# A batched matrix product: weights cast to bfloat16 by their own transfers instead of by VectorE and ScalarE

## The chip, the cores and the metric

The kernel runs on one NeuronCore of a Trainium2 chip. The metric is the device time of one execution in microseconds; inputs and output lie in the chip's main memory (HBM), in float32, before and after. A core has five engines that run on their own and meet at semaphores: PE (TensorE, matrix products), DVE (VectorE), ACT (ScalarE), POOL (GpSimd) and SP (SyncE, which issues transfers here). Sixteen DMA engines carry out the transfers.

## The reference

```python
b1, b2, m, k, n = 8, 16, 256, 512, 384
x      = np.random.randn(b1, b2, m, k).astype(np.float32)
weight = np.random.randn(b1, b2, k, n).astype(np.float32)

def reference(x, weight):
    return np.matmul(x, weight).astype(np.float32)
```

These are 128 independent products of a 256 x 512 with a 512 x 384 matrix. x has 67.1 MB, weight 100.7 MB, the result 50.3 MB.

## The kernel before

The 128 products are taken in 32 groups (NG) of four (G). The matrix products are computed from bfloat16 copies of x and weight, with sums in float32.

**x.** One transfer of 2048 KB (load_x, L104) brings a group's four matrices of 256 x 512 into x_sb, 128 partitions with eight rows of 512 each: partitions 0 to 31 hold the first matrix, and so on. There are two such buffers. In four steps of two rows (T = 4, the index q in the code) DVE casts them to x_bf (cast_x, L142), which has one buffer; PE transposes x_bf into PSUM, two bfloat16 values taken as one 32-bit word (transpose, L193); ACT copies the transposed words to x_t (evacuate, L183), which has two buffers.

**Weights.** One transfer of 3072 KB (load_w, L116) brings a group's four matrices into w_sb as float32, with 16 adjacent rows (24 KB) in each partition: partitions 0 to 31 hold the first matrix. There are two buffers. Each matmul needs a whole matrix spread over 128 partitions, four rows in each. So the casts to w_bf also move data between partitions: 16 casts for a group (cast_w, L154), each from 32 partitions with 4 rows to 32 other partitions. DVE does 11 of them (CV) and ACT 5 (CA). w_bf holds two groups. In the first four groups and the last two ("short" groups, is_short, L113) a group comes in two transfers of 1536 KB with 8 rows in each partition, and DVE alone makes 8 casts of 64 partitions (cast_short, L167).

Since the rows of a matrix fall on partitions in another order this way (which row of K stands where), cast_x writes the columns of x in a matching order: its output or input is rearranged by S = 4, or S = 2 in the short groups.

**Products.** For each step q PE multiplies two sets of rows (multiply, L208): the four matrices of a group use 32 columns of the array each, and four matmuls follow one another over K. That is 128 matmuls of 384 columns in a group, into one of two PSUM buffers (po). ACT copies po to out_sb (copy_out, L228), four buffers; one transfer of 1536 KB stores a group (store, L132).

**Order.** The order of every engine is written out by hand.

- SP issues all transfers from one queue (on_sync, L244): first x and weights of four groups (LAG), then for each group: load_x of group n + 4, store of group n, load_w of group n + 4. A load waits until the casts of the group two earlier have freed its buffer: L108 waits for x_cast, L120 and the line behind it for w_vcast and w_acast.
- DVE (on_vector, L266) takes for each group 8 weight casts, the four x casts of the next group, and the last 3 weight casts.
- PE (on_tensor, L294) transposes group n + 1, then multiplies group n.
- ACT (on_scalar, L309) evacuates the transposes of group n + 1, then copies group n's results out in four steps with 5 weight casts of group n + 1 between them.
- POOL (on_gpsimd, L238) makes the identity matrix for the transposes and has nothing else to do.

Of the kernel before, what the change touches and what calls it, by code (L numbers as in the profile page):

```python
# [12 lines left out]
def kernel(  # L13
# [6 lines left out]
    nc = tc.nc  # L20
    P = 128
# [20 lines left out]
    C = P // G  # L42
    R = G * M // P
    T = R // 2
    SH, SL = 2, 4
    NG = B // G

    XS, WS, OS = 2, 2, 4
    BS, TS, WBS = 1, 2, 2 * G
    PT, PO = 4, 2  # L50

    LAG = 4

    CA = 5
    CV = G * SL - CA
    HV = G * SH

    XV = 8

    ctx.enter_context(tc.tile_critical(no_gpsimd_drain=True))  # L60

# [10 lines left out]
    def sems(name, n):  # L72
        return [tc.alloc_semaphore(f"{name}{s}") for s in range(n)]
# [4 lines left out]

    x_bf = sbuf("x_bf", [P, R, K], bf16, BS)
    x_t = sbuf("x_t", [P, R, KO // 2, P, 2], bf16, TS)  # L80
    w_sb = sbuf("w_sb", [P, SL * KO, N], fp32, WS)
    w_bf = sbuf("w_bf", [P, KO, N], bf16, WBS)
    out_sb = sbuf("out_sb", [P, R, N], fp32, OS)
    pt = psum("pt", [P, 2, KO // 2, P], fp32, PT)
    po = psum("po", [P, 2, 512], fp32, PO)
# [1 line left out]

    id_done, x_cast, w_vcast, w_acast, t_made, t_copied, p_made, o_copied = (  # L90
        sems(name, 1)[0]
        for name in (
            "id_done", "x_cast", "w_vcast", "w_acast",
            "t_made", "t_copied", "p_made", "o_copied",
        )
    )
    x_in, w_in, o_out = sems("x_in", XS), sems("w_in", WS), sems("o_out", OS)
    h_in = sems("h_in", G)


    BIAS = 8
# [8 lines left out]
            x_rows[bass.ds(n * (G * M), G * M)].rearrange("(p r) k -> p r k", r=R),  # L110
        ).then_inc(x_in[s % XS], 16)

    def is_short(n):  # L113
        return isinstance(n, int) and (n < LAG or n >= NG - 2)

    def load_w(e, t, U, s):  # L116
        n = t * U + s
        if not isinstance(n, int) or n >= WS:
            e.wait_ge(w_vcast, n * CV + (1 - WS) * CV)
            e.wait_ge(w_acast, n * CA + (1 - WS) * CA)  # L120
        d = SL // SH if is_short(n) else 1
        k = SL * KO // d
        for h in range(d):
            sem = h_in[s % WS * 2 + h] if is_short(n) else w_in[s % WS]
            e.dma_start(  # L125
                w_sb[s % WS][:, h * k : (h + 1) * k, :],
                w_rows[bass.ds(n * (G * K) + h * (G // d * K), G // d * K)].rearrange(
                    "(p k) n -> p k n", k=k
                ),
            ).then_inc(sem, 16)  # L130

    def store(e, t, U, s, pieces=1):  # L132
        n = t * U + s
# [8 lines left out]
    def cast_x(e, t, U, s, q):  # L142
        n = t * U + s
        if q == 0:
            e.wait_ge(x_in[s % XS], (t * (U // XS) + s // XS) * 16 + 16)
        e.wait_ge(t_made, n * T + (q + 1 - T + BIAS))  # L146
        rows = slice(2 * q, 2 * q + 2)
        S = SH if is_short(n) else SL
        e.tensor_copy(  # L149
            out=x_bf[s % BS][:, rows].rearrange("p r (s q c) -> p r s q c", s=S, c=KO),  # L150
            in_=x_sb[s % XS][:, rows].rearrange("p r (q s c) -> p r s q c", s=S, c=KO),
        ).then_inc(x_cast, 1)

    def cast_w(e, t, U, s, parts, first=True):  # L154
        n = t * U + s
        if first:
            e.wait_ge(p_made, n * T + (BIAS - T))
            e.wait_ge(w_in[s % WS], (t * (U // WS) + (s - LAG) // WS) * 16 + 16)  # L158
        copy = e.tensor_copy if e is nc.vector else e.copy
        for c in parts:  # L160
            i, h = c // SL, c % SL
            copy(  # L162
                out=w_bf[(s * G + i) % WBS][h * C : (h + 1) * C],
                in_=w_sb[s % WS][i * C : (i + 1) * C, h * KO : (h + 1) * KO, :],
            ).then_inc(w_vcast if c < CV else w_acast, 1)

    def cast_short(e, n):  # L167
        e.wait_ge(p_made, n * T + (BIAS - T))
        p = P // SH
        for d in range(SL // SH):  # L170
            turns = n // WS if n < LAG else LAG // WS
            e.wait_ge(h_in[n % WS * 2 + d], turns * 16 + 16)  # L172
            for a in range(SH):
                for h in range(SH):
                    c = d * 4 + a * 2 + h
                    r = (d * SH + h) * KO

                    e.tensor_copy(  # L178
                        out=w_bf[(n * G + d * SH + a) % WBS][h * p : (h + 1) * p],
                        in_=w_sb[n % WS][a * p : (a + 1) * p, r : r + KO, :],  # L180
                    ).then_inc(w_vcast, 2 if c < CV - HV else 1)

    def evacuate(e, t, U, s):  # L183
        n = t * U + s
# [22 lines left out]

    def multiply(e, t, U, s):  # L208
        n = t * U + s
        e.wait_ge(w_acast, n * CA + CA)  # L210
        e.wait_ge(w_vcast, n * CV + CV)
        for q in range(T):
            e.wait_ge(t_copied, n * T + (q + 1 + BIAS))
            e.wait_ge(o_copied, n * T + (q + 1 - PO + BIAS))
            for rr in range(2):
                for ko in range(KO):
                    for i in range(G):
                        mine = slice(i * C, (i + 1) * C)
                        ins = e.matmul(  # L219
                            po[(s * T + q) % PO][mine, rr, :N],  # L220
                            x_t[s % TS][:, 2 * q + rr, ko // 2, mine, ko % 2],
                            w_bf[(s * G + i) % WBS][:, ko, :],
                            start=(ko == 0),
                            stop=(ko == KO - 1),
                        )
            ins.then_inc(p_made, 1)
# [11 lines left out]
    def on_gpsimd(e):  # L238
# [2 lines left out]
        make_identity(nc, identity[:], nomemset=True)  # L241
        e.drain().then_inc(id_done, 1)

    def on_sync(e):  # L244
        U = OS
        for n in range(LAG):
            load_x(e, 0, NG, n)
            load_w(e, 0, NG, n)
        rounds = (NG - 2 - LAG) // U
        with e.Fori(0, rounds) as t:  # L250
            for s in range(U):
                load_x(e, t, U, LAG + s)
                store(e, t, U, s)
                load_w(e, t, U, LAG + s)

        for n in range(LAG + rounds * U, NG):
            load_x(e, 0, NG, n)
            if n < NG - 1:
                store(e, 0, NG, n - LAG)
            load_w(e, 0, NG, n)  # L260
        for n in range(NG - 1 - LAG, NG):
            store(e, 0, NG, n, T if n == NG - 1 else 1)
        for s in range(OS):
            e.wait_ge(o_out[s], 16 + 16 * (NG // OS + (T - 1 if s == (NG - 1) % OS else 0)))

    def on_vector(e):  # L266
        U = 2

        def next_x(t, U, s):
            for q in range(T):  # L270
                cast_x(e, t, U, s + 1, q)

        def step(t, U, s):
            n = t * U + s
            if is_short(n):
                cast_short(e, n)
            else:
                cast_w(e, t, U, s, range(XV))
            if not isinstance(n, int) or n < NG - 1:
                next_x(t, U, s)  # L280
            if not is_short(n):
                cast_w(e, t, U, s, range(XV, CV), False)

        next_x(0, NG, -1)
        for n in range(LAG):
            step(0, NG, n)
        rounds = (NG - 3 - LAG) // U
        with e.Fori(0, rounds) as t:  # L288
            for s in range(U):
                step(t, U, LAG + s)  # L290
        for n in range(LAG + rounds * U, NG):
            step(0, NG, n)

    def on_tensor(e):  # L294
        U = 2
        e.sem_inc(t_made, BIAS)
        e.sem_inc(p_made, BIAS)
        e.wait_ge(id_done, 2)
# [1 line left out]

        pe = mybir.EngineType.PE
        with nc.Fori(0, NG // U, engines=OrderedEngineSet([pe]), head_slot={pe: 0}) as t:
            transpose(e, t, U, 1)
            multiply(e, t, U, 0)
            with e.If(t < NG // U - 1):
                transpose(e, t, U, 2)
            multiply(e, t, U, 1)

    def on_scalar(e):  # L309
        U = OS  # L310
# [4 lines left out]

        def step(t, U, s):
            short = is_short(t * U + s + 1)
            evacuate(e, t, U, s + 1)  # L320
            for q in range(T):
                copy_out(e, t, U, s, q)
                if q == 0 and short:
                    e.sem_inc(w_acast, CA)
                if q > 0 and not short:
                    last = CA if q == T - 1 else q
                    cast_w(e, t, U, s + 1, range(CV + q - 1, CV + last), q == 1)

        evacuate(e, 0, NG, 0)
        e.sem_inc(w_acast, CA)  # L330
        for n in range(LAG - 1):
            step(0, NG, n)
        rounds = (NG - 2 - LAG) // U
        with e.Fori(0, rounds) as t:
            for s in range(LAG - 1, LAG - 1 + U):
                step(t, U, s)
        for n in range(LAG - 1 + rounds * U, NG - 1):
            step(0, NG, n)
        for q in range(T):
            copy_out(e, 0, NG, NG - 1, q)  # L340

    on_gpsimd(nc.gpsimd)
    on_sync(nc.sync)
    on_vector(nc.vector)
    on_tensor(nc.tensor)
# [31 lines left out]
```

## Time and profile before

| | |
|---|---|
| time, median of 2 runs | 518.49 us (518.36 to 518.61) |
| profiled execution: span from the first to the last instruction | 516.8 us |
| granted clock of PE, mean over the span | 0.780 of full speed |
| busy: PE / DVE / ACT / POOL | 315.2 / 397.7 / 410.3 / 0.7 us |
| DMA: moved / rate over the span | 218.19 MB / 422 GB/s |
| transfers: weights, x, results | 26 of 3072 KB and 12 of 1536 KB, 32 of 2048 KB, 31 of 1536 KB and 4 of 384 KB |

The profile is of one execution, and its own time is the span; the runs of the first row were timed apart from it, and their median is 1.7 us more. Busy time is the time in which an engine executes; an engine can be idle because it waits, which is no harm unless all the rest waits for it. The trace also records each packet that a DMA engine moves, with its size and the time that it took; here a packet is one contiguous run of one partition. In the groups of instructions a line such as "L162 DVE CAST w_bf<-w_sb 32x1536 bf16<-32x1536 f32 x286 | 271.9, 951 | 81.6" is to be read: line 162 of the kernel, executed by DVE, a cast from w_sb to w_bf of 32 partitions by 1536 values, 286 times, 271.9 us in all, 951 ns each, and 81.6 us idle ahead of them.

### The profile page before, as it was taken

Reading aid. Unit: us, or ns where it says so; the run is one execution under the profiler, and the core shown is the slowest. Engines: PE = TensorE matmul, PEld = TensorE weight load, DVE = VectorE, ACT = ScalarE, POOL = GpSimd, SP = SyncE. Lnnn points to the kernel's source line nnn. Section 1 sums busy time; section 2 is a strip of 40 time slices with the busy share of each in tenths; the row PEclk is TensorE's granted clock in tenths of the full one; section 3 lists DMA queues with packets and bytes.
Section 4 is the critical chain, followed back from the end, with each engine's and each line's share of the span. In section 5 each row is a group of like instructions: output and inputs, shape, how many; then the busy total and the mean of one; then the engine's idle time right before and its main releaser. Section 6 shows DMA issues by size and latency. Waiting matters only on the chain.

```text
span 516.8 us, 11572 instructions
## 1 busy us (share of the span) xinstructions
PE 315.2 (61%) x4608; PEld 225.4 (44%) x4608; DVE 397.7 (77%) x462; ACT 410.3 (79%) x387; POOL 0.7 (0%) x6
## 2 busy tenths in 40 slices
PE   2277838555676675765475766558656667565681
PEld 2255525444454443454353544435534445344550
DVE  2788757798777897777987778977779777797960
ACT  1365666998797989798979879978989897899561
POOL 0000000000000000000000000000000000000000
PEclk9687786878786778787778868776867786688887
DMA  8999999999999999999999999999999999999995
GB/s 335 426 428 425 435 429 423 431 430 434 429 424 431 432 439 434 424 426 433 434 434 431 422 432 433 435 429 428 425 438 429 440 428 420 433 433 429 424 428 219
DMA packets 15127, 218.19 MB, mean 422 GB/s; under 512 B 1680, under 2 KB 1680, under 8 KB 2192
## 3 DMA queue, kind: packets, MB, share of 16 engines
q1 hardware_dynamic: 15120, 218.11, 99.0%
q8 instruction: 3, 0.05, 0.0%
q14 instruction: 4, 0.03, 0.0%
HBM read 167.77 MB, written 50.33 MB: 422 GB/s over the span
## 4 chain that ended last, share of the span: by engine, by line
DMA 57%; DVE 29%; issue 9%; PE 1%; SPq 1%; DVEq 1%; ACT 0%
DMA w_sb<-in_weight_dram 57%; DVE w_bf L162 20%; DVE x_bf L149 5%; DVE w_bf L178 4%; PE po L219 1%; SPq L125 0%; DVEq L288 0%; SPq L108 0%; DVEq L158 0%; ACT out_sb L233 0%; SPq L120 0%; DVEq L146 0%; DVEq L172 0%; SPq L372 0%; SPq L60 0%
## 5 line engine op out<-in xcount | busy, mean ns | idle before, releaser
L162 DVE CAST w_bf<-w_sb 32x1536 bf16<-32x1536 f32 x286 | 271.9, 951 | 81.6 <-DMA w_sb<-in_weight_dram 73.5
L219 PE MATMUL po<-w_bf,x_t 128*32 128x384 bf16 x4096 | 200.6, 359 | 38.3 <-DVE w_bf L162 21.0
L201 PE MATMUL pt<-identity,x_bf 128*128 128x128 f32 x512 | 115.0, 415 | 152.2 <-DVE x_bf L149 152.2
L162 ACT CAST w_bf<-w_sb 32x1536 bf16<-32x1536 f32 x130 | 190.9, 1468 | 6.0 <-DMA w_sb<-in_weight_dram 2.8
L201 PEld LDWEIGHTS pt<-identity,x_bf 128*128 128x128 f32 x512 | 103.4, 224 | 164.1 <-issue 163.8
L219 PEld LDWEIGHTS po<-w_bf,x_t 128*32 128x32 bf16 x4096 | 122.0, 106 | 115.9 <-issue 40.7
L233 ACT COPY out_sb<-po 128x768 f32<-128x768 f32 x128 | 101.5, 803 | 57.3 <-PE po L219 56.6
L188 ACT COPY x_t<-pt 128x1024 bf16<-128x1024 bf16 x128 | 120.3, 1025 | 22.1 <-PE pt L201 21.5
L149 DVE CAST x_bf<-x_sb 128x1024 bf16<-128x1024 f32 x128 | 80.0, 688 | 12.4 <-DMA x_sb<-in_x_dram 11.5
L178 DVE CAST w_bf<-w_sb 64x1536 bf16<-64x1536 f32 x48 | 45.9, 955 | 8.3 <-DMA w_sb<-in_weight_dram 7.0
L188 ACT ACT_TABLE_LOAD x1 | 1.3, 1283 | 10.8 <-PE pt L201 10.8
masks.py:199 POOL TENSOR_SCALAR_AFFINE_SELECT identity<-identity 128x128 f32<-128x128 f32 x1 | 0.3, 294 | 0.2 <-POOL identity L239 0.2
L239 POOL MEMSET identity<- 128x128 f32 x1 | 0.2, 205 | 0.5 <-SPq L60 0.5
L361 POOL MEMSET const-bfloat16-1.0<- 128x1 bf16 x1 | 0.1, 102 | 0.0
L361 POOL MEMSET const-uint8-127<- 128x1 uint8 x1 | 0.1, 102 | 0.0
L361 POOL MEMSET const-float32-0.0<- 128x1 f32 x1 | 0.1, 99 | 0.2 <-issue 0.2
L361 POOL MEMSET const-float32-1.0<- 128x1 f32 x1 | 0.1, 99 | 0.0
## 6 DMA issues: line engine op xcount, KB each, us to landing
w_sb<-in_weight_dram SPq DMA_DIRECT2D x26, 3072.0 KB, 18.1
x_sb<-in_x_dram SPq DMA_DIRECT2D x32, 2048.0 KB, 22.3
out_dram<-out_sb SPq DMA_DIRECT2D x31, 1536.0 KB, 25.4
w_sb<-in_weight_dram SPq DMA_DIRECT2D x12, 1536.0 KB, 16.6
out_dram<-out_sb SPq DMA_DIRECT2D x4, 384.0 KB, 5.6
```

The source lines that it names most:

```text
L149: e.tensor_copy(out=x_bf[s % BS][:, rows].rearrange("p r (s q c) -> p r s q c", s=S, c=KO), in_=x_sb[s % XS][:, rows].rearrange("p r (q s ...
L162: copy(out=w_bf[(s * G + i) % WBS][h * C : (h + 1) * C], in_=w_sb[s % WS][i * C : (i + 1) * C, h * KO : (h + 1) * KO, :],).then_inc(w_vcas ...
L178: e.tensor_copy(out=w_bf[(n * G + d * SH + a) % WBS][h * p : (h + 1) * p], in_=w_sb[n % WS][a * p : (a + 1) * p, r : r + KO, :],).then_inc ...
L188: e.copy(out=x_t[s % TS][:, 2 * q : 2 * q + 2], in_=pt[(s * T + q) % PT][:].bitcast(bf16),).then_inc(t_copied, 1)
L201: ins = e.transpose(pt[(s * T + q) % PT][:, rr, h, :], words[:, 2 * q + rr, h :: KO // 2], identity[:],)
L219: ins = e.matmul(po[(s * T + q) % PO][mine, rr, :N], x_t[s % TS][:, 2 * q + rr, ko // 2, mine, ko % 2], w_bf[(s * G + i) % WBS][:, ko, :], ...
L233: e.copy(out=out_sb[s % OS][:, 2 * q : 2 * q + 2, :], in_=po[(s * T + q) % PO][:, :, :N],).then_inc(o_copied, 1)
L239: e.memset(identity[:], 0.0).then_inc(id_done, 1)
L361: nc = _bacc.Bacc("TRN2", target_bir_lowering=False, num_devices=1)
```

## The change

Weight transfers are issued from GpSimd, and source and destination differ in type: they read float32 from HBM and write bfloat16 into w_bf. w_sb and all weight casts of DVE and ACT are gone, and with them the short groups. w_bf is one tensor for a group, 128 partitions with four rows of each of the four matrices, in two buffers; partition p holds rows 4p to 4p + 3 of each matrix. Since that is the order in which x has its columns, cast_x casts without rearranging. load_w of group n + 2 waits until PE has finished the products of group n; GpSimd issues all 32 after it has made the identity matrix. multiply waits for the transfer's semaphore instead of the casts'. On SP the loop now has the store of group n, then load_x of group n + 4.

```diff
-    XS, WS, OS = 2, 2, 4
-    BS, TS, WBS = 1, 2, 2 * G
+    XS, OS = 2, 4
+    BS, TS, WBS = 1, 2, 2
...
-    w_sb = sbuf("w_sb", [P, SL * KO, N], fp32, WS)
-    w_bf = sbuf("w_bf", [P, KO, N], bf16, WBS)
+    w_bf = sbuf("w_bf", [P, G, KO, N], bf16, WBS)
...
+    def load_w(e, n):
+        if n >= WBS:
+            e.wait_ge(p_made, (n + 1 - WBS) * T + BIAS)
+        e.dma_start(
+            w_bf[n % WBS][:],
+            w_rows[bass.ds(n * (G * K), G * K)].rearrange("(g p k) n -> p g k n", g=G, p=P),
+        ).then_inc(w_in[n % WBS], 16)
...
-        S = SH if is_short(n) else SL
-        e.tensor_copy(
-            out=x_bf[s % BS][:, rows].rearrange("p r (s q c) -> p r s q c", s=S, c=KO),
-            in_=x_sb[s % XS][:, rows].rearrange("p r (q s c) -> p r s q c", s=S, c=KO),
-        ).then_inc(x_cast, 1)
+        e.tensor_copy(out=x_bf[s % BS][:, rows], in_=x_sb[s % XS][:, rows]).then_inc(x_cast, 1)
...
     def multiply(e, t, U, s):
         n = t * U + s
-        e.wait_ge(w_acast, n * CA + CA)
-        e.wait_ge(w_vcast, n * CV + CV)
+        e.wait_ge(w_in[s % WBS], (t * (U // WBS) + s // WBS) * 16 + 16)
...
-                            w_bf[(s * G + i) % WBS][:, ko, :],
+                            w_bf[s % WBS][:, i, ko, :],
...
+    def load_all_w(e):
+        for n in range(NG):
+            load_w(e, n)
...
     def on_sync(e):
         U = OS
         for n in range(LAG):
             load_x(e, 0, NG, n)
-            load_w(e, 0, NG, n)
-        rounds = (NG - 2 - LAG) // U
+        rounds = (NG - LAG) // U
         with e.Fori(0, rounds) as t:
             for s in range(U):
+                store(e, t, U, s)
                 load_x(e, t, U, LAG + s)
-                store(e, t, U, s)
-                load_w(e, t, U, LAG + s)
...
     def on_vector(e):
         U = 2
+        with e.Fori(0, NG // U) as t:
             for s in range(U):
+                for q in range(T):
+                    cast_x(e, t, U, s, q)
...
+        evacuate(e, 0, NG, 0)
+        rounds = (NG - U) // U
+        with e.Fori(0, rounds) as t:
+            for s in range(U):
+                evacuate(e, t, U, s + 1)
+                for q in range(T):
+                    copy_out(e, t, U, s, q)
...
     on_gpsimd(nc.gpsimd)
+    load_all_w(nc.gpsimd)
```

More of the change, by code (lines that the diff above doesn't have):

```diff
@@ L44 @@
     T = R // 2
-    SH, SL = 2, 4
     NG = B // G
-    XS, WS, OS = 2, 2, 4
-    BS, TS, WBS = 1, 2, 2 * G
+    XS, OS = 2, 4
+    BS, TS, WBS = 1, 2, 2
     PT, PO = 4, 2
     LAG = 4
[L54 to L58, printed above, removed]
     ctx.enter_context(tc.tile_critical(no_gpsimd_drain=True))
@@ L85 @@
     po = psum("po", [P, 2, 512], fp32, PO)
-    id_done, x_cast, w_vcast, w_acast, t_made, t_copied, p_made, o_copied = (
+    id_done, x_cast, t_made, t_copied, p_made, o_copied = (
         sems(name, 1)[0]
         for name in (
-            "id_done", "x_cast", "w_vcast", "w_acast",
+            "id_done", "x_cast",
             "t_made", "t_copied", "p_made", "o_copied",
@@ L96 @@
     )
-    x_in, w_in, o_out = sems("x_in", XS), sems("w_in", WS), sems("o_out", OS)
-    h_in = sems("h_in", G)
+    x_in, w_in, o_out = sems("x_in", XS), sems("w_in", WBS), sems("o_out", OS)
     BIAS = 8
@@ L111, in load_x @@
         ).then_inc(x_in[s % XS], 16)
[L113 to L130, printed above, removed]
+    def load_w(e, n):
[5 more added lines that the diff above has]
+        ).then_inc(w_in[n % WBS], 16)
     def store(e, t, U, s, pieces=1):
@@ L147, in cast_x @@
         rows = slice(2 * q, 2 * q + 2)
-        S = SH if is_short(n) else SL
-        e.tensor_copy(
-            out=x_bf[s % BS][:, rows].rearrange("p r (s q c) -> p r s q c", s=S, c=KO),
-            in_=x_sb[s % XS][:, rows].rearrange("p r (q s c) -> p r s q c", s=S, c=KO),
-        ).then_inc(x_cast, 1)
[L154 to L181, printed above, removed]
+        e.tensor_copy(out=x_bf[s % BS][:, rows], in_=x_sb[s % XS][:, rows]).then_inc(x_cast, 1)
     def evacuate(e, t, U, s):
@@ L247, in on_sync @@
             load_x(e, 0, NG, n)
-            load_w(e, 0, NG, n)
-        rounds = (NG - 2 - LAG) // U
+        rounds = (NG - LAG) // U
         with e.Fori(0, rounds) as t:
             for s in range(U):
+                store(e, t, U, s)
                 load_x(e, t, U, LAG + s)
-                store(e, t, U, s)
-                load_w(e, t, U, LAG + s)
[L256 to L261, printed above, removed]
+        for n in range(NG - LAG, NG):
             store(e, 0, NG, n, T if n == NG - 1 else 1)
@@ L267, in on_vector @@
         U = 2
[L269 to L288, printed above, removed]
+        with e.Fori(0, NG // U) as t:
             for s in range(U):
-                step(t, U, LAG + s)
-        for n in range(LAG + rounds * U, NG):
-            step(0, NG, n)
+                for q in range(T):
+                    cast_x(e, t, U, s, q)
     def on_tensor(e):
-        U = 2
+        U = WBS
         e.sem_inc(t_made, BIAS)
@@ L302, in on_tensor @@
         with nc.Fori(0, NG // U, engines=OrderedEngineSet([pe]), head_slot={pe: 0}) as t:
-            transpose(e, t, U, 1)
-            multiply(e, t, U, 0)
+            for s in range(U - 1):
+                transpose(e, t, U, s + 1)
+                multiply(e, t, U, s)
             with e.If(t < NG // U - 1):
-                transpose(e, t, U, 2)
-            multiply(e, t, U, 1)
+                transpose(e, t, U, U)
+            multiply(e, t, U, U - 1)
     def on_scalar(e):
@@ L314, in on_scalar @@
             e.sem_inc(o_out[s], 16)
-        def step(t, U, s):
-            short = is_short(t * U + s + 1)
-            evacuate(e, t, U, s + 1)
-            for q in range(T):
[L322 to L340, printed above, removed]
+        evacuate(e, 0, NG, 0)
[5 more added lines that the diff above has]
+                    copy_out(e, t, U, s, q)
+        for n in range(rounds * U, NG):
+            if n < NG - 1:
+                evacuate(e, 0, NG, n + 1)
+            for q in range(T):
+                copy_out(e, 0, NG, n, q)
     on_gpsimd(nc.gpsimd)
+    load_all_w(nc.gpsimd)
     on_sync(nc.sync)
```

## The prediction

> **What bounds the kernel now.** I read the page's share of the DMA queues first, then the table of windows, then the chain of waits, and last the groups of instructions. The queue part of the page:
>
> ```profile
> q1 hardware_dynamic: 15120, 218.11, 99.0%
> HBM read 167.77 MB, written 50.33 MB: 422 GB/s over the span
> ```
>
> The reader is to see 99.0%: all loads and stores run on one queue, and their packets fill the 16 DMA engines for 0.99 of 516.8 us. The bytes are exactly those of x, weight and out; nothing is moved twice. The windows say where the missing 1% lies (columns: window, its length, busy us and count of each engine, clock, DMA share, GB/s):
>
> ```profile
> 0.00:20.00 20.00, 3.46 (x16) 3.28 (x16) 8.61 (x11) 5.04 (x5) 0.70 (x6) 0.90 0.91 366
> 200.00:300.00 100.00, 59.14 (x894) 43.02 (x884) 82.59 (x96) 90.26 (x84) 0.00 (x0) 0.79 1.01 432
> 500.00:517.00 17.00, 5.39 (x128) 3.77 (x128) 0.10 (x1) 3.20 (x4) 0.00 (x0) 0.83 0.63 262
> ```
>
> DMA stands at 1.01 in the middle (full), 0.91 in the first 20 us (1.8 us lost) and 0.63 in the last 17 us (6.3 us lost). The chain of waits seems to say something else:
>
> ```profile
> DMA 57%; DVE 29%; issue 9%; PE 1%; SPq 1%; DVEq 1%; ACT 0%
> ```
>
> 29% of it is DVE, because SP issues a weight load only when the casts have freed w_sb, so the chain passes through casts. But while those casts run the DMA engines have other transfers, which the window row of 1.01 shows. A cast that vanishes therefore gives its time to nobody. The groups that the change removes or touches (busy us, mean ns, idle before):
>
> ```profile
> L162 DVE CAST w_bf<-w_sb 32x1536 bf16<-32x1536 f32 x286 | 271.9, 951 | 81.6 <-DMA w_sb<-in_weight_dram 73.5
> L162 ACT CAST w_bf<-w_sb 32x1536 bf16<-32x1536 f32 x130 | 190.9, 1468 | 6.0 <-DMA w_sb<-in_weight_dram 2.8
> L149 DVE CAST x_bf<-x_sb 128x1024 bf16<-128x1024 f32 x128 | 80.0, 688 | 12.4 <-DMA x_sb<-in_x_dram 11.5
> L178 DVE CAST w_bf<-w_sb 64x1536 bf16<-64x1536 f32 x48 | 45.9, 955 | 8.3 <-DMA w_sb<-in_weight_dram 7.0
> ```
>
> **The price of a packet.** The trace records every DMA packet with its size and time. Medians: 3072 B in 121 ns, 12288 B in 460, 16384 B in 612, 24576 B in 912. From the first and the second, 9216 B take 339 ns, 27.2 B per ns; what is left is 8 ns a packet (24576 / 27.2 + 8 = 912, as recorded). Loads and stores lie on the same line. A group is four matrices, and there are 32. Its share of the work on each of the 16 engines: 8 packets of x (16 KB, mean 618 ns) 4.94 us, 8 of a store (12 KB) 3.70 us, 8 of weights (24 KB) 7.30 us: 15.9 us, which is the distance of successive weight loads in the timeline (210.51 and 226.41 us).
>
> **Casts removed.** 271.9 + 45.9 us of DVE and 190.9 us of ACT go. DVE keeps 80 us, ACT 222 us (120.3 + 101.5), of a span of over 500. Neither bounded; gain 0. What remains per group is PE: 315.2 / 32 = 9.9 us, under 16. Were the DMA work to vanish, PE would be next, at about 9.9 x 32 = 317 us.
>
> **x cast in its own order.** The same 128 casts of 128x1024; the order within a row changes. Its price lies between half of 688 ns and twice that; 2.75 us a group or 5.5, both beside 16 us of DMA. 0.
>
> **Weight transfers.** 26 transfers of 3072 KB and 12 of 1536 KB become 32 of 3072 KB, read as before, but written as bfloat16, half the bytes. A partition now takes four consecutive rows of each of four matrices: a run of 4 x 384 x 4 = 6144 B read and 3072 B written, where a run was 24 KB (12 KB in the short groups). So 3328 packets of 912.5 ns and 1536 of 462 ns (3.746 ms, by 16 engines 234.1 us) give way to 32 x 512 = 16384 packets. No packet of the trace casts, so the price of one is bounded by rows: if only the written bytes count, 121 ns (the row of 3072 B), 123.9 us in all, 110 us less; if the read bytes count, 6144 / 27.2 + 8 = 234 ns, 239.6 us, 5.5 us more (only the 8 ns of more packets); if reading and writing follow each other, 234 + 121 = 355 ns, 363.5 us, 129 us more. I take 234 ns: the line of the rows goes by the bytes that an engine has to stream, in both directions alike, and all 6144 still have to be read.
>
> **Issue from GpSimd.** POOL has 0.7 us of work now, ahead of the first load: memset, identity, drain. So weights start about 1 us later than SP's first at 1.41 us; two x loads (4.9 us each) cover that. The issue takes 0.33 us on SP for 128 runs; for 512 at the same rate 1.3 us. No row shows GpSimd at this, so its cost runs from there to the point where one issue lasts a group's 16.1 us; below that it is hidden behind the load issued before. It no longer stands in SP's row: there load_x now follows the store of four groups earlier, so it also waits for the last copy of that group. x has two buffers and its cast runs one group ahead; the 25.3 us median from a store's issue to landing already lies in a full queue. 0.
>
> **Two weight buffers, freed later.** w_bf now has two buffers, and load n+2 waits for the last matmul of group n, queued behind nothing but other weight loads. Within two periods (32.2 us) must fit: its issue (1.3 us or more), its landing and one group's matmuls (7.17 us in the slow stretch of the clock at 210 us). Landing: even if each packet of weights let one of SP's through, the whole group is through after 16.1 us. 1.3 + 16.1 + 7.2 = 24.6, so 7.6 us to spare for a backlog. The added wait costs 0; if that cover is gone, each group loses what is over 7.6 us.
>
> **Head and tail.** The first matmuls stood at 26.65 us behind the casts and the second x; now w0 and x1 are enough, some 5 us earlier, with no gain, since the engines have x and weights to move all the while. At the end, the 5.9 us of six casts between the last weights and the last matmuls vanish, but stores of the groups before fill that stretch now (0.63). I count 0, with 3 us either way.
>
> **Sum.** DMA busy 99.0% of 516.8 is 511.7 us (the packets' times, added and divided by 16, give the same); 511.7 - 234.1 + 239.6 = 517.2; idle 5.1 as before: span 522.3. The median of the runs, 518.49, stands 1.7 us above the profiled span; the same added: **524.0 us**, 1% slower. I take 2% (10.4 us) as what a measurement of this kernel tells from no change. With head and tail, 516 to 531.
>
> **The rivals.**
> (1) *The written bytes set the packet's time.* 121 ns: 511.7 - 234.1 + 123.9 = 401.5, + 6.8 = **408 us**. The period is then 12.5 us, and the two-buffer loop still fits (1.3 + 12.5 + 7.2 = 21 of 25). For it: loads end in SBUF at the same rate as stores leave it, so a limit at SBUF fits the rows too. Against: the stores' rows show the same limit at both ends, and the reading end is unchanged. Faster by over 2% from 218 ns a packet down. [...] Chance 0.14.
> (2) *Casting packets are slower*: an engine that converts doesn't overlap the reading of one run with the writing of the one before. 355 ns: 511.7 - 234.1 + 363.5 + 6.8 = **648 us**, slower. It is slower by over 2% already from 239 ns a packet (10.4 - 5.5 us over 1024 packets per engine is 4.8 ns more). For it: 1024 conversions per engine where there were none, and no cover, at 99%. Against: plain packets lose only 8 ns each. Chance 0.26.
> (3) *The runs are cut finer*, to one row of 384: 65536 packets of 1536 / 27.2 + 8 = 64.5 ns, 264.2 us, **549 us**. Against: the four rows of a partition are adjacent at both ends, as the 16 now are. Chance 0.08.
> (4) *GpSimd can't issue fast enough.* Each load is 512 runs, four times SP's. If one issue takes over 16.1 us (31 ns a run, twelve times SP's rate), it sets the period; at 20 us 32 x 20 + 20 = **660 us**. [...] No row of before shows GpSimd issuing. Chance 0.08.
> That the change doesn't do what it says is excluded by w_sb being gone: the matmuls read what the transfer wrote.
>
> **How the numbers follow.** Forecast 0.44, and the rivals 0.14, 0.26, 0.08, 0.08. Faster is (1): 0.14. Slower are (2), (3), (4) and the forecast's upper edge (0.03): 0.45. Same: 0.41. The range leaves out (1) and the far end of (2) and (4), about 0.2: 514 to 660. The forecast's own is 516 to 531.
>
> **What would show it.** In the profile after: packets of the new queue with a mean of 234 ns (121, 355 or 64 for the rivals); DMA at 1.0 in the middle; DVE near 80 and ACT near 222 us; PE's matmuls waiting on weights in DMA rather than on casts; weight loads landing within 24 us. DMA windows clearly under 1.0 would prove me wrong on the issue or on the two buffers; a full DMA and another time, on the packet.

## The result and the profile after

The changed kernel takes 555.93 us (median of 2 runs, 552.63 to 559.24), against 518.49 us before: 1.0724 of the time, with an interval of 1.0686 to 1.0763. The profiled execution took 552.63 us with a span of 550.8 us. The forecast was 524.0 us; the kernel is 32 us slower than that. Ratios and their intervals, here and below, come from fast runs alone; one run of "load n still issued after group n - 2" and one of "no cast" fell in a slower state, and these two count only in the median and the range given there.

The page of the changed kernel, its queues and bytes, then the groups of instructions that the prediction named:

```profile
q1 hardware_dynamic: 9648, 117.44, 51.4%
q0 software_dynamic: 16896, 50.33, 48.6%
HBM read 167.77 MB, written 50.33 MB: 396 GB/s over the span
...
L165 PE MATMUL po<-w_bf,x_t 128*32 128x384 bf16 x4096 | 222.2, 387 | 237.9 <-DMA w_bf<-in_weight_dram 234.7
...
L128 DVE CAST x_bf<-x_sb 128x1024 bf16<-128x1024 f32 x128 | 81.7, 700 | 435.5 <-DMA x_sb<-in_x_dram 249.4
L135 ACT COPY x_t<-pt 128x1024 bf16<-128x1024 bf16 x128 | 120.5, 1037 | 3.4 <-PE pt L148 3.4
...
L107 POOL DMA_DIRECT2D w_bf<-in_weight_dram x32 | 23.8, 745 | 498.4 <-PE po L165 489.5
```

The weights now have a queue of their own (q0; its 50.33 MB are the written bytes), and HBM is read as much as before. The weight casts are gone: DVE is left with 81.7 us, and ACT with 219.9. Matmuls wait 234.7 us for weights, and GpSimd waits 489.5 us for matmuls before it may issue the next weights. SP has little to add in the meantime, because it waits as well, for the copies of the results that it is to store:

```profile
SPq L118 <- ACT out_sb L179: 486.0, 35, 26.5
```

The two queue shares add up to 100%, which looks like full DMA engines. They are not full. The packets are recorded with overlapping times, so shares over 1 occur (1.07 and 1.03 in two of the windows below), and they cover up gaps. Three windows of the changed kernel (window, its length, busy us and count of each engine, clock, DMA share, GB/s; for the casting packets the GB/s count written bytes only):

```profile
199.00:206.00 7.00, 7.00 (x112) 3.79 (x116) 0.00 (x0) 1.90 (x3) 0.00 (x0) 0.62 1.07 238
206.00:210.00 4.00, 4.00 (x68) 3.05 (x64) 2.35 (x4) 3.50 (x5) 0.74 (x1) 1.00 0.43 36
210.00:238.00 28.00, 13.62 (x248) 8.78 (x244) 2.79 (x5) 10.52 (x13) 0.74 (x1) 0.76 1.03 336
```

For 4 us the share is 0.43, with 36 GB/s moved: the engines have run out of work. The chain of waits of the changed kernel, in order of time (start, length, what), shows the loop that leads there:

```profile
170.60 28.14 DMA w_bf<-in_weight_dram
198.95 8.02 PE po L165 x103
206.97 0.28 issue
207.26 23.58 DMA w_bf<-in_weight_dram
231.05 7.34 PE po L165 x101
238.39 0.28 issue
238.68 27.79 DMA w_bf<-in_weight_dram
```

A weight load lands, the matmuls of that group run, the end of the matmuls lets GpSimd issue the load two groups later, and so on. From 170.60 to 238.68 us are 68.1 us for four groups, 17.0 us a group where the DMA work of a group is 16.1 by the forecast's sum.

To size the gaps I added up, from the packet records, the bytes that each microsecond starts to stream (the read bytes of a casting packet), as a share of 16 engines at 27.2 B per ns. I call a microsecond under 0.7 starved. Leaving out the first 20 and the last 25 us, the changed kernel has 41 microseconds under 0.7; together they fall 27 us short of the 0.971 that holds on average elsewhere. The kernel before has one such microsecond, 0.3 us short.

### The profile page after: what moved, and what is told of

The parts are those of the page before. It is cut to its first block, busy times and chain, and to the rows that moved or that the text cites. A ratio compares the mean times of both kernels' runs of the same rounds, so it can differ in the third digit from the quotient of the medians.

```text
span 550.8 us, 10930 instructions
## 1 busy us (share of the span) xinstructions
PE 292.4 (53%) x4608; PEld 196.7 (36%) x4608; DVE 81.7 (15%) x128; ACT 219.9 (40%) x257; POOL 24.5 (4%) x38
## 3 DMA queue, kind: packets, MB, share of 16 engines
q0 software_dynamic: 16896, 50.33, 48.6%
HBM read 167.77 MB, written 50.33 MB: 396 GB/s over the span
## 4 chain that ended last, share of the span: by engine, by line
DMA 74%; PE 22%; issue 2%; ACT 1%; POOLq 0%; POOL 0%; SPq 0%
DMA w_bf<-in_weight_dram 74%; PE po L165 22%; ACT x_t L135 1%; ACT out_sb L179 0%; POOLq L188 0%; POOL identity L185 0%; POOLq masks.py:199 0%; POOLq L285 0%; SPq L53 0%
## 5 line engine op out<-in xcount | busy, mean ns | idle before, releaser
L165 PE MATMUL po<-w_bf,x_t 128*32 128x384 bf16 x4096 | 222.2, 387 | 237.9 <-DMA w_bf<-in_weight_dram 234.7
L165 PEld LDWEIGHTS po<-w_bf,x_t 128*32 128x32 bf16 x4096 | 130.3, 113 | 323.5 <-issue 267.9
L128 DVE CAST x_bf<-x_sb 128x1024 bf16<-128x1024 f32 x128 | 81.7, 700 | 435.5 <-DMA x_sb<-in_x_dram 249.4
L148 PE MATMUL pt<-identity,x_bf 128*128 128x128 f32 x512 | 72.7, 298 | 15.0 <-DVE x_bf L128 15.0
L148 PEld LDWEIGHTS pt<-identity,x_bf 128*128 128x128 f32 x512 | 66.4, 210 | 24.7 <-issue 24.7
L107 POOL DMA_DIRECT2D w_bf<-in_weight_dram x32 | 23.8, 745 | 498.4 <-PE po L165 489.5
## 6 DMA issues: line engine op xcount, KB each, us to landing
x_sb<-in_x_dram SPq DMA_DIRECT2D x32, 2048.0 KB, 16.9
w_bf<-in_weight_dram POOLq DMA_DIRECT2D x32, 1536.0 KB, 24.8
```

Of the source, the lines that this page charges most:

```text
L107: e.dma_start(w_bf[n % WBS][:], w_rows[bass.ds(n * (G * K), G * K)].rearrange("(g p k) n -> p g k n", g=G, p=P),).then_inc(w_in[n % WBS], 16)
L128: e.tensor_copy(out=x_bf[s % BS][:, rows], in_=x_sb[s % XS][:, rows]).then_inc(x_cast, 1)
L148: ins = e.transpose(pt[(s * T + q) % PT][:, rr, h, :], words[:, 2 * q + rr, h :: KO // 2], identity[:],)
L165: ins = e.matmul(po[(s * T + q) % PO][mine, rr, :N], x_t[s % TS][:, 2 * q + rr, ko // 2, mine, ko % 2], w_bf[s % WBS][:, i, ko, :], start= ...
```

## The experiments

Two theories for the lost time. **Gaps** (A): the loop over two weight buffers leaves the engines without work. **Price** (B): the records give a casting packet 261 ns on average, where the forecast had 234; 1024 such packets per engine make 27 us, which is also about the loss.

**Four weight buffers.** The changed kernel with

```diff
-    BS, TS, WBS = 1, 2, 2
+    BS, TS, WBS = 1, 2, 4
```

> The changed kernel with four weight buffers (WBS 4) instead of two; nothing else differs but that the loop of PE is unrolled over four groups. Theory A (gaps): the two-buffer loop leaves the DMA engines without work; in the trace of the changed kernel weight packets that run alone start 70 to 72 times per us on 16 engines, so 225 ns apart per engine, which is 6144 B at 27.2 B/ns, and there are stretches of some 3 us with hardly a packet about every 68 us. With loads issued two groups earlier these stretches go: DMA full, 512 to 524 us. Theory B (price): a casting packet costs the 261 ns that its records show on average, against 234 forecast, and the engines were full in the changed kernel too (97 to 100% of the span by queue): the sum does not change with buffers, 545 to 556 us.

Measured: 523.9 us (523.06 to 524.79), 1.01 of before (1.0083 to 1.0118). The gaps are gone: no microsecond under 0.7. A stretch of 100 us in it, the matmuls' wait for weights, and the answer on the tile w_bf (issue to landing):

```profile
200.00:300.00 100.00, 54.67 (x896) 38.23 (x899) 17.89 (x28) 45.28 (x53) 5.18 (x7) 0.79 1.04 330
...
PE po L165 <- DMA w_bf<-in_weight_dram: 210.6, 25, 15.4
...
DMA to landing us min/median/max: 29.5/55.1/70.0
```

A load now takes 55.1 us to land instead of 24.8, and the kernel is 32 us faster: the 30 us more that a load lies queued cost nothing here, since it was issued early enough. The matmuls' wait for weights is nearly what it was, 210.6 us against 234.7: it is there in both, with gaps and without, and so it does not show the loss. B falls: it had 545 to 556 us here, whatever the buffers. The casting packets' median is 247 ns in both kernels; their mean went from 261 to 247 ns only because the long ones (499 packets over 300 ns, 680 ns each on average) are gone but for 8.

**Four buffers, load n still issued after group n - 2.** The four buffers and

```diff
-        if n >= WBS:
-            e.wait_ge(p_made, (n + 1 - WBS) * T + BIAS)
+        if n >= 2:
+            e.wait_ge(p_made, (n + 1 - 2) * T + BIAS)
```

> Four weight buffers as in the run with four, and the same unrolled loop of PE, but load n still waits until group n-2 has been multiplied, so no load is issued earlier than in the changed kernel. It tells the earlier issue from the place of the buffers and the longer loop. Theory A: as the changed kernel, 548 to 560 us. If the longer loop or other addresses were what helps the run with four buffers: as fast as that one. Theory B: 545 to 556 us, as every version.

Measured: 558.6 us (554.41 to 564.61), 1.0717 (1.0689 to 1.0744), with 37 starved microseconds. It is the time of the issue that counts, not the place of the buffers or PE's longer loop.

**Three loads in flight** (the same edit with 3 for 2).

> Four weight buffers, but load n waits until group n-3 has been multiplied: three loads in flight at most. The loop then has three periods, 48.3 us, for issue, landing and matmuls. With three loads queued a load lands later than 24.4 us, but at most two and a half groups of work lie ahead (40 us) and 8 us of matmuls follow: it just fits. Theory of gaps: as four buffers, 522 to 530 us; were four needed, 530 to 545 us.

Measured: 526.1 us (524.66 to 526.39), 1.0138 (1.0121 to 1.0155); a load lands in 40.5 us (median), and two microseconds are starved. One load more in flight takes back all but some 2 us.

**x ahead of the store on SP**, two weight buffers.

```diff
-                store(e, t, U, s)
                 load_x(e, t, U, LAG + s)
+                store(e, t, U, s)
```

> The changed kernel with two weight buffers, but on SP load_x of group n+4 ahead of the store of group n, as in the kernel before. Theory A in the form that the weights' wait alone makes the gaps: little changes, 540 to 558 us. Theory A in the form that the gaps need x to stand behind the store too (x could fill them if it were issued as soon as its buffer is free): 520 to 535 us. Theory B: 545 to 556 us.

Measured: 556.87 us (556.70 to 557.86), 1.0747 (1.0729 to 1.0765), 43 starved microseconds. The order on SP has no part in it.

**No cast**, two weight buffers: w_bf as float32, the matmuls read the upper halves.

```diff
-    w_bf = sbuf("w_bf", [P, G, KO, N], bf16, WBS)
+    w_bf = sbuf("w_bf", [P, G, KO, N], fp32, WBS)
...
-                            w_bf[s % WBS][:, i, ko, :],
+                            w_bf[s % WBS][:].bitcast(bf16)[:, i, ko, 1::2],
```

> The changed kernel with weight transfers that do not cast: float32 to float32, same runs of 6144 B, same queue, same two buffers and waits; the matmuls read the upper 16 bits of each float32 word, so weights are truncated to bfloat16 instead of rounded. Theory A: the cast costs nothing beside the bytes read, the gaps stay: 545 to 560 us, packets alone again about 225 to 234 ns apart. Theory B: plain packets cost 234 ns, and the time falls to 520 to 530 us. If the casting packet were cheaper than a plain one (half the bytes written), the time would rise over 560 us.

Measured: 550.3 us (546.63 to 554.89), 1.0562 (1.054 to 1.0584). The gaps stay without any cast (35 starved microseconds, 21 us short), which is against B. By the ratios it is 1.5% faster than the changed kernel (1.0562 against 1.0724); with gaps in both, this run does not say what that is, so the price of the cast was measured again with full engines, below.

**Why a load takes so long to land.** The prediction had 16.1 us. This is what the queues moved while a weight load, stores and x were all under way (218 to 224 us of the changed kernel), and, in the second fence, with weights alone (201 to 206 us):

```profile
q1 hardware_dynamic: 126, 1.85, 73.7%
q0 software_dynamic: 123, 0.38, 31.6%
```

```profile
q0 software_dynamic: 350, 1.08, 108.5%
q1 hardware_dynamic: 3, 0.00, 0.1%
```

Of the 126, 13 are the semaphores' of 4 B; that leaves 113 packets of x against 123 of weights. With a store under way the counts are as even: 89 packets of the store against 92 of weights between 213 and 217 us. So the engines took the two queues in turn here, one packet each, although SP's had 16 or 12 KB and the weights' read 6 KB, and weights got less than a third of the engines while SP had x to move (31.6% against 73.7% of recorded packet time). A turn is one recorded packet: between 213 and 217 us the rate rises from 154 to some 600 GB/s and falls again every 0.7 us, which is one packet of weights and one of a store (226 + 460 ns). Alone, 350 packets in 5 us are 21.9 per engine, one every 229 ns.

How late a load gets by such turns depends on what the queues hold. These are the issues around the load of 207.26 us (start, length):

```profile
207.26 0.74 POOL L107 DMA_DIRECT2D w_bf<-in_weight_dram  x1 [23.19 <-PE po L165]
...
207.98 0.35 SPq L118 DMA_DIRECT2D out_dram<-out_sb  x1
208.62 0.34 SPq L99 DMA_DIRECT2D x_sb<-in_x_dram  x1
...
215.40 0.74 POOL L107 DMA_DIRECT2D w_bf<-in_weight_dram  x1 [7.40 <-PE po L165]
...
216.12 0.35 SPq L118 DMA_DIRECT2D out_dram<-out_sb  x1
216.76 0.34 SPq L99 DMA_DIRECT2D x_sb<-in_x_dram  x1
```

The load lands at 230.84 us. By the packet records 23 packets of SP's pass on each engine, on average, before its last one is through: the 16 of the first store and x, and 7 of the second. The load of 215.40 stands behind it in the same queue, and its first packet starts only at 229.76 us.

To test the turns, each x load and each store was cut in two halves of the rows, which wait for the same things as before (the semaphores' counts follow):

```diff
-        e.dma_start(
-            x_sb[s % XS][:],
-            x_rows[bass.ds(n * (G * M), G * M)].rearrange("(p r) k -> p r k", r=R),
-        ).then_inc(x_in[s % XS], 16)
+        dram = x_rows[bass.ds(n * (G * M), G * M)].rearrange("(p r) k -> p r k", r=R)
+        for h in range(2):
+            rows = slice(h * R // 2, (h + 1) * R // 2)
+            e.dma_start(x_sb[s % XS][:, rows], dram[:, rows]).then_inc(x_in[s % XS], 16)
...
-    def store(e, t, U, s, pieces=1):
+    def store(e, t, U, s, pieces=2):
...
```

> The changed kernel with two weight buffers, but each x load and each store is issued as two transfers of half the rows, both after the same waits, so SP's packets have 8 and 6 KB instead of 16 and 12. The theory of gaps says why 24.8 us pass from a weight load's issue to its landing where the prediction had 16.1: an engine takes packets of the two queues in turn, one for one, whatever their size, and the 32 packets of one load per engine meet the 32 packets of SP from two groups, not the 16 of one. 32 x 226 ns + 16 x 460 + 16 x 612 = 24.4 us. With half packets the 32 of a load meet one group's: 32 x 226 + 16 x 309 + 16 x 234 = 15.9 us; the loop then fits into two periods, the gaps go, and the time is that of the four buffers plus 16 more packets a group of 8 ns, 4 us: 524 to 534 us. If turns don't matter and only the sum of the work does, the gaps stay: 552 to 566 us.

Measured: 531.37 us (531.11 to 532.20), 1.0254 (1.0237 to 1.0271), with two weight buffers and the unchanged wait. The same work, more finely cut, is 25 us faster than the changed kernel. The DMA issues of this run (KB each, median us to landing), and the window in which the changed kernel was empty:

```profile
x_sb<-in_x_dram SPq DMA_DIRECT2D x64, 1024.0 KB, 26.2
w_bf<-in_weight_dram POOLq DMA_DIRECT2D x32, 1536.0 KB, 22.5
...
206.00:210.00 4.00, 1.60 (x8) 1.61 (x9) 2.43 (x4) 0.44 (x1) 0.00 (x0) 0.77 1.06 309
```

Weights now land in 22.5 us and x in 26.2, where the changed kernel had 24.8 and 16.9: the weights' share has grown at x's cost. No microsecond is starved. 22.5 us is more than the 15.9 expected. A load's own packets do take 15.8 us from the first to the last (median), as expected; 4 to 9 us pass ahead of the first one, in which the load ahead in the queue is mostly not through. With 7 to 8 us of matmuls it still fits into two periods. The 7.5 us over the four buffers are 4 us of packets more, as expected, and some 3 us that stay unexplained.

**The price of a cast, with full engines.** For room, two result buffers instead of four (OS = 2) with four weight buffers; then the same without the cast.

> Four weight buffers and two buffers for the results instead of four, to make room for the next run, which it is to be compared with. A copy into a buffer now waits for the store of two groups before; a store lands 11 us after its issue in the changed kernel, under two periods of 16 us. 522 to 532 us.

> The same with two result buffers and four weight buffers, and weight transfers that do not cast (float32 to float32, the matmuls read the upper 16 bits of each word, so weights are truncated instead of rounded). The DMA engines are full in both, so the difference is the price of the cast: if a casting packet costs its read bytes, 234 ns against a plain one's 234, the two times agree within 1% (5 us, or 5 ns a packet over 1024 packets per engine); if the records' 247 ns against 234 were real time, the cast would be 13 us slower; if the written bytes eased anything, the cast would be the faster one by more than that.

Measured: 526.21 us (523.72 to 527.68; 1.014, interval 1.0105 to 1.0174) with the cast and 528.74 us (526.03 to 529.77; 1.018, interval 1.0151 to 1.0209) without. The intervals overlap and the cast is not the slower one. The records say 247 ns for the casting packet (3072 B written) and 234 for the plain one (6144 B written), in the median; the 13 ns don't show in the time. That fits records that overlap: in microseconds with weights alone, the first run starts 69 packets and the second 68 on 16 engines, one every 232 and 235 ns. Half the written bytes gained no more than about 1% here.

## Why the prediction was wrong

- **What bounds the kernel**: right, as far as it goes. Full DMA engines (a share of 1.04 from 200 to 300 us) set 523.9 us with four buffers, and the 508.7 us of casts on DVE and ACT that vanished gave nothing against 518.49.
- **The packet at 234 ns**: right. The sum was 524.0 us and four buffers give 523.9; that sum holds the 5.5 us for more packets, and it is what the change costs with full engines. That it fits to 0.1 us is luck: the runs differ more than that among themselves (523.06 to 524.79). The sign named for it, a mean record of 234 ns, did not come: it is 261 ns in the changed kernel and 247 with four buffers. Rival 1 (written bytes, 408 us) and rival 2 (read and write one after the other, 648 us) are refuted by the pair with and without the cast. Half the weights' bytes written moved the time by about 1% at most; what sets the 27.2 B per ns, no run here tells. Rival 3 is out: q0 has 16896 packets, 16384 and the semaphores', not 65536.
- **Issue from GpSimd**: right, and 745 ns instead of 1.3 us. No issue of the changed kernel took over 0.88 us, so rival 4 is out.
- **x cast** 700 ns against 688, **order on SP** worth nothing: both right.
- **Head**: wrong, but the sum counted nothing for it. The first matmuls came at 32.1 us, not 5 us ahead of 26.65: w0, issued at 2.35 us, took 29.5 us, since it shared turns with the first four x loads, and 31 of their 32 packets per engine passed until it was through (32 x 226 + 32 x 612 ns = 26.8 us for all of both).
- **Two weight buffers, freed later**: this is the step that failed, in its term for the landing. It put in 16.1 us; measured are 24.8 in the median, and 28.1 and 23.6 in turn in the chain above. "Even if each packet of weights let one of SP's through, the whole group is through after 16.1 us" had the turns right but only one group's 16 packets on SP's side. SP's queue gets the next group's store and x before the load is through, and 23 packets pass in the median of all loads, up to 31. And a load that is "queued behind nothing but other weight loads" waits for the one ahead of it, for which the prediction put in nothing: in the stretch with gaps, the first packet of every second load starts 11 to 15 us after its issue. (The sum 32 packets against 32, 24.4 us, comes near the median of 24.8 in part by luck: it has too many of SP's packets and no wait in the queue.)

What the landing costs can be read from the chain. From one issue into a buffer to the next pass 36.7 us (from 170.60) and 31.4 us (from 207.26), 34.0 on average, where two periods are 32.2. That is 1.8 us too much for two groups, 0.9 us a group and 29 us in 32 groups; the spans of the changed kernel and of the one with four buffers differ by 28.0 us (550.8 and 522.8). The prediction's rule that each group loses what is over 7.6 us charges twice what the loop loses, since one turn of a buffer covers two groups: with the median's 8.7 us over 16.1 it would give 1.1 us a group, 35 us in all, which is near the 32 us lost by chance. The matmuls have a small part as well: 8.0 and 7.3 us in the chain where 7.2 was put in, at a clock of 0.62 in the window from 199 to 206 us. The last group's took 5.41 us, where the clock is 0.93 (535 to 551 us); with that a turn would be some 31.7 us and just fit, an estimate that no run here tests.

The condition stood in the text; the number put into it was too small, and its failure got no rival with a chance of its own. The sign "slower" had a chance of 0.45, but for mechanisms that did not act, and the wide range of 514 to 660 us holds 555.93 for their sake alone: that is luck, as is the nearness of rival 3's 549 us. The sign that the prediction set for this failure, "DMA windows clearly under 1.0", is not to be seen in windows of 100 us (1.00 to 1.04), only in windows of a few.

## What to carry to other kernels

When a transfer moves to a second queue, look in the trace for turns, and work out the landing time from them. Here a load passed one packet for each packet of the other queue (123 against 113 between 218 and 224 us), so the queue of small packets got the smaller share (31.6% against 73.7%), and all that the other queue was given until then counted, later groups' work too (23 packets an engine in the median instead of one group's 16). What still stood ahead in its own queue came on top (the first packet of every second load 11 to 15 us after its issue). Then check that issue, landing and the work that frees the buffer fit into as many periods as there are buffers. Here two periods of 16.1 us were missed by 1.8 us, and more buffers (523.9 us with four, 526.1 with three loads in flight) or finer packets on the other queue (531.37 us) took back most of the 32 us; where they fit by less than a few microseconds, try one of these. With the DMA engines full, the casts on DVE and ACT were free here (518.49 us with them, 523.9 with casting transfers and four buffers), and a cast in the transfer won nothing with the read bytes unchanged (526.21 us with it, 528.74 without).

## What the runs showed that was not expected

A casting packet of 6144 B read and 3072 B written is recorded with 247 ns, yet alone such packets follow each other every 229 ns on an engine: shares of DMA engines made from packet records go up to 1.09 in a window, and two queue shares that add up to 100% went with 27 us of starved engines.

The packets just after a gap were slow: 491 of the 499 casting packets over 300 ns start in a starved microsecond or within 6 us after one. The 27 us hold this slow start too, so a gap cost more here than the time in which nothing moves. DVE casts x just then (207.65 to 210.28 us at the gap shown), but neither that nor the cast in the transfer is needed for it: in the kernel before, the first 16 packets of x take 1.4 us each on average, against 0.61 later, some 6 us ahead of DVE's first cast. Why the first packets into idle engines were slow stays open.
